# An MLP with seven products a pair: five stage tiles, other request points for weights and blocks, weight sums tied to a bank's addition, operands made one product ahead

## The chip, the core and the metric

The kernel runs on one core of one Trainium2 chip. The metric is the device time of one execution in microseconds (us); several executions give a median. A profile of one execution is read beside it.

## What is computed

The reference is a chain of layers on 1024 tokens of width 1024: a sliding-window attention layer, a pooling layer, then a block with neighbourhood attention and a gated linear recurrence, and at the end of that block an MLP and a norm. The change touches what comes after the recurrence, that is the last lines:

```python
mix = jax.nn.sigmoid(gate_na) * y_na + jax.nn.sigmoid(gate_hg) * y_hg
h = h + mix @ w_o[l]
m = rms_norm(h, norm_mlp[l])
h = h + jnp.square(jax.nn.relu(m @ w_up[l])) @ w_down[l]      # w_up 1024x4096, w_down 4096x1024
h = rms_norm(h, norm_final)
```

All is float32. A product of two float32 matrices is made of three TensorE passes: each operand is split into a high part (a cast on ScalarE) and a low part (operand less high part), and high x high, high x low and low x high are added in a bank of PSUM.

## The kernel before

**The up-projection.** The tokens are halved (Xa, Xb: 512 each), the 1024 input features are halved, and the 4096 output features are taken as 16 pairs of 2 x 128. A pair is a 2x2 matrix product of blocks and is made with seven products in place of eight: A11, A12, S2, S1, S3, S4, A22. Each is four contraction steps of three matmuls 128x128x512, so 12 matmuls, 84 a pair. The activations are ready once for all pairs (`xx`: the parts A11, A12, A22, S1; `sh`: S2 to S4, made by `sums(j)`, L1441 to L1461, from transposes of Xb). For each pair the weights r1 and r2 (raw, 128 x 8 x 128 each) come by DMA (`raws`, L1485); VectorE makes four sums of halves of them (`vec`, L1479: first r2 in place, then the two halves of `tt`, last half of r1 in place); `split_group` (L1470 to L1476) splits r1, tt, r2 and the rest of r1 on ScalarE (`whi`, L1474, ring of three tiles) and GpSimd (`wlo`, L1475). S2 and S1 use tt, S3 and S4 use r2, A22 uses r1's second half, A11 and A12 use all of r1 as it came.

**What follows a product.** A bank is copied out to a stage tile (`copy_out`, ScalarE, L1390), a later bank is added to that tile (`add_bank`, VectorE, L1394), relu and square are two passes of ScalarE (`activated`, L1411 and L1412), and the result goes to DRAM. So u11 = A11, plus A12; u12 = S2's bank plus S4's; u22 = S1's bank plus S3's; u21 = A22's bank. S3 goes on in the bank that u12's copy is read from, so it waits for that copy (L1390); A22 goes on in the bank that u22's addition reads (L1394). At the end of `pair` four sums of u's are made by VectorE (L1479, st<-st) and stored by SyncE's queue (L1518 to L1524) for the second matrix product. Stage tiles are a ring of ten.

**The order.** The code of a pair stands in one order, a scheduler sets the order of instructions on each engine. On VectorE the pieces of one pair stand so: four u sums of the pair before; u11's addition; four weight sums of the next pair; u22's addition; u12's addition. Each engine runs its queue in order, so the weight sums, when their DMA is late, hold up u22's addition. The raw weights of pair p+2 are asked for at the end of `pair(p)`, ahead of its four stores in the code; the tiles must be free.

Pairs 0 to 3 have A11 and A12 early (`first_two` between the `sums(j)`), so their run is five products each. Ahead of all this, GpSimd adds high and low parts of Xa's transposed half back to float32 (eight additions into `fa`, L1432), and `norms(6, 2)` normalises the last of Xb.

**The down-projection.** Four chunks of seven products, 48 matmuls each (`times`). `split_a` and `split_b` make the operands (L117, L118), `less` differences of weights (L1600), `into` adds four banks to X in SBUF (L1640). In the code a product's `into` stands ahead of the next product's operands.

Of the kernel before, what the change touches and what calls it, by code (L numbers as in the profile page):

```python
# [8 lines left out]
F32 = mybir.dt.float32  # L9
# [9 lines left out]
P = 128  # L19
# [10 lines left out]
def fused_kernel(tc, a, out, stop=None, dbg=None):  # L30
# [1262 lines left out]
    xa, xb = x0p.tile([P, 4, D], F32, name="Xa"), x1p.tile([P, 4, D], F32, name="Xb")  # L1293
# [10 lines left out]
    def bank():  # L1304
        return psm.tile([P, 512], F32, name="mm")
# [17 lines left out]

    with ExitStack() as ph:
        gp = ph.enter_context(tc.tile_pool(name="gp", bufs=2))

        def mixed(e):

            mx, wh = [], pair_cols(w_hg, e)
            for i in range(2):  # L1330
                m_h = gp.tile([P, T], F32R, name="mh", bufs=4)
                m_l = gp.tile([P, T], F32R, name="ml", bufs=4)
                mx.append((m_h, m_l))
                for hf in range(2):
                    sl = slice(hf * 512, hf * 512 + 512)
                    sg = []
                    for src in (d_gate[8 + e + i], d_y[e + i]):
                        g_ = gp.tile([P, 512], F32, name="sg", bufs=8)
# [16 lines left out]
        def last_hook(t):  # L1355
            nc.sync.dma_start(out=d_x[t], in_=X[ALL, t, slice(0, D)])
            if t == 5:
                norms(0, 4)
            if t == 6:
                transposed(lambda k: bank(), [X[ALL, i, slice(0, D)] for i in range(4)], g_mlp, xx, 0)  # L1360
# [25 lines left out]
    H0, H1 = slice(0, 512), slice(512, 1024)  # L1386

# [4 lines left out]

    def add_bank(c_, ps):
        nc.vector.tensor_tensor(out=c_, in0=c_, in1=ps, op=ALU.add)  # L1394
        return c_

    with ExitStack() as ph:
# [29 lines left out]
        fa = xa.rearrange("p t (a c) -> p (t a) c", a=2)  # L1427
# [7 lines left out]
        def turned(k):  # L1435
            ps = bank()
            for i in range(4):
                nc.tensor.transpose(ps[:, i * P:(i + 1) * P], xb[:, i, k * P:(k + 1) * P], ident)
            return ps

        def sums(j):  # L1441

            pa, pb = turned(j), turned(4 + j)
# [15 lines left out]
            split_evac(sh[3][0][:, j, :], sh[3][1][:, j, :], s3, nc.gpsimd)  # L1459
            nc.vector.tensor_tensor(out=s2, in0=fa[:, 4 + j, :], in1=s2, op=ALU.subtract)  # L1460
# [24 lines left out]
        def raws(p):  # L1485
            rs = [wp2.tile([P, KT, P], F32, name="raw") if p else raw() for _ in range(2)]
            for r_, i in zip(rs, (0, 1)):
                nc.sync.dma_start(out=r_, in_=cols(w_up, (2 * p + i) * P)[1])
            return rs

        def pair(p, r1, r2):
# [4 lines left out]
            vec(r2[:, lo_], r2[:, lo_], r2[:, hi_], ALU.subtract)  # L1496
            vec(tt[:, lo_], r1[:, lo_], r2[:, lo_], ALU.subtract)
            vec(tt[:, hi_], r2[:, hi_], tt[:, lo_], ALU.subtract)
            vec(r1[:, hi_], r1[:, hi_], tt[:, lo_], ALU.subtract)
# [18 lines left out]
            nc.sync.dma_start(out=d_u["S3"][:, p, :], in_=s3)  # L1518
            s1 = vec(u21, u21, u22, ALU.add)
            nc.sync.dma_start(out=d_u["S1"][:, p, :], in_=s1)  # L1520
            s2 = vec(stage(), u22, s3, ALU.add)
            nc.sync.dma_start(out=d_u["S2"][:, p, :], in_=s2)
            s4 = vec(stage(), u12, s2, ALU.subtract)
            nc.sync.dma_start(out=d_u["S4"][:, p, :], in_=s4)  # L1524
            return nxt

        rs = {0: raws(0), 1: raws(1)}
        for p in range(NPR):
            rs[p + 2] = pair(p, *rs.pop(p))


    with ExitStack() as ph:
# [3 lines left out]
        blocks = [xa[:, 2 * i:2 * i + 2, :].rearrange("p t (a c) -> p (t a) c", a=2) for i in range(2)]  # L1536
# [28 lines left out]
        NCH = NPR // 4  # L1565
        wd = w_dn.rearrange("(q j p) c -> p q j c", j=2, p=P)
        seq = [(c, s_) for c in range(NCH) for s_ in ("A11", "A12", "S2", "S1", "S4", "S3", "A22")]

        def load_a(n):
            if n < len(seq):  # L1570
                c, s_ = seq[n]
                nc.sync.dma_start(out=blocks[n % 3], in_=d_u[s_][:, 4 * c:4 * c + 4, :])

        def load_w(dst, j, n, c):
            for i in range(2):
                q = 4 * c + 2 * i
                nc.sync.dma_start(out=dst[i], in_=wd[:, q:q + 2, j, n * 512:n * 512 + 512])
            return dst

        def load_w11(c):  # L1580
            return load_w([wpool.tile([P, 1024], F32, name="wraw", bufs=3).rearrange("p (k c) -> p k c", k=2)
                           for _ in range(2)], 0, 0, c)

        def load_w21(c):
            return load_w([bb.tile([P, 2, 512], F32, name="wb") for _ in range(2)], 1, 0, c)

        def load_w2(c):
            wx = xt.tile([P, KT, 512], F32, name="xh1")
            w12, w22 = [[wx[:, 4 * n + 2 * i:4 * n + 2 * i + 2, :] for i in range(2)] for n in range(2)]
            load_w(w22, 1, 1, c)  # L1590
            load_w(w12, 0, 1, c)
            return w12, w22
# [33 lines left out]
        load_a(0)  # L1626
        w11 = load_w11(0)
        load_a(1)
# [6 lines left out]
        load_x(1, 0)  # L1635
        for c in range(NCH):
            def into(banks, h, ch, done=False):
                for t in range(4):
                    dst = X[:, 4 * h + t, ch * 512:ch * 512 + 512]
                    nc.vector.tensor_tensor(out=dst, in0=dst, in1=banks[t], op=ALU.add)  # L1640
                    if done and c == NCH - 1:
                        half_done(4 * h + t, ch)
                        if ch == 1 - h:
                            finish(4 * h + t)

            n = 7 * c
            B, A_, C = [[bank() for _ in range(4)] for _ in range(2)] + [None]
            times(B, split_a(n), split_b(w11), True)
            into(B, 0, 0)
            less(w12, w12, w22)  # L1650
            times(A_, split_a(n + 1), split_b(w21), True)
            into(A_, 0, 0, True)
# [4 lines left out]
            less(w11, w22, w11)  # L1657
            C = [bank() for _ in range(4)]
            times(C, split_a(n + 3), split_b(w11), True)
            into(C, 1, 1)  # L1660
            if c < NCH - 1:
# [4 lines left out]
            times(C, split_a(n + 4), split_b(w22), False)  # L1666
            into(C, 0, 1, True)
            times(B, split_a(n + 5), split_b(w12), False)
            into(B, 1, 1, True)
            if c < NCH - 1:  # L1670
                w12, w22 = load_w2(c + 1)
            times(B, split_a(n + 6), split_b(w21), False)
            into(B, 1, 0, True)
            if c < NCH - 1:
                w21 = w21_
    ctx.close()
# [25 lines left out]
```

## Time and profile before

| | us |
|---|---|
| median of three executions (2424.01 to 2425.98) | 2425.92 |
| the profiled execution | 2424.15 |
| its span in the profile | 2422.1 |
| TensorE (PE) busy | 2328.9 (96%) |
| VectorE (DVE) busy | 1438.3 (59%) |
| ScalarE (ACT) busy | 954.0 (39%) |
| GpSimd (POOL) busy | 770.0 (32%) |
| mean granted TensorE clock | 0.992 |

The profiled execution's time is 2.05 us longer than its span, and 1.8 us under the median. Matmuls overlap, so a busy share of 96% is not 96% of the peak: the distance between the starts of two matmuls is what counts.

### The profile page before, as it was taken

To read this page: it belongs to the slowest core of one execution; us is meant where nothing else is said; L and a number is where in the kernel's file an instruction comes from. 1 tells how busy PE (TensorE), PEld (TensorE's weight loads), DVE (VectorE), ACT (ScalarE), POOL (GpSimd) and SP (SyncE) were. 2 spreads that over 40 slices of the span, in tenths; PEclk is the share of its full clock that TensorE was granted. 3 is DMA by queue.
4 is the path that set the end of the run, shared out by engine and by line. 5 is a ranking of instruction groups with operands and counts; after the bars stand their busy time and mean duration, and the time that the engine had idled before them with its cause. 6 is when DMAs were issued, how large, how long until landed. Compare 5 with 4: busy or idle time off the path is not lost. (4 is left out here: it accounts for less than half of the span.)

```text
span 2422.1 us, 32164 instructions
## 1 busy us (share of the span) xinstructions
PE 2328.9 (96%) x12102; PEld 1930.0 (80%) x12102; DVE 1438.3 (59%) x2647; ACT 954.0 (39%) x1783; POOL 770.0 (32%) x519
## 2 busy tenths in 40 slices
PE   8999999999999999999999999999889899899997
PEld 7877778888877888889888888888767777788885
DVE  5566676644457255552474655766864444687776
ACT  5344451422226355542333323322554444433334
POOL 2111132121235443331221211112554344444454
PEclk9999999999999999999999999999999999999999
DMA  5111113111114311211112112663344444754231
GB/s 157 36 27 36 27 36 106 31 57 44 57 61 140 82 47 53 55 61 45 53 36 66 44 44 74 199 236 105 130 152 161 138 140 140 267 193 174 98 120 70
DMA packets 234012, 230.01 MB, mean 95 GB/s; under 512 B 59833, under 2 KB 174863, under 8 KB 230273
## 3 DMA queue, kind: packets, MB, share of 16 engines
q1 hardware_dynamic: 225040, 210.31, 27.3%
q10 hardware_dynamic: 8224, 16.00, 1.8%
q0 software_dynamic: 592, 1.65, 0.3%
q8 instruction: 95, 1.56, 0.3%
q14 instruction: 61, 0.49, 0.1%
HBM read 168.68 MB, written 59.24 MB: 94 GB/s over the span
## 5 line engine op out<-in xcount | busy, mean ns | idle before, releaser
L107 PE MATMUL mm<-xh,whi 128*128 128x512 f32 (+2 forms) x1744 | 673.1, 386 | 18.1 <-DVE st L1394 13.4
L109 PE MATMUL mm<-xl,whi 128*128 128x512 f32 (+2 forms) x1744 | 666.3, 382 | 0.0
L110 PE MATMUL mm<-xh,wlo 128*128 128x512 f32 (+2 forms) x1744 | 663.0, 380 | 2.0 <-POOL wlo L79 2.0
L79 POOL TENSOR_TENSOR wlo<-wraw,whi 128x1024 fp32r<-128x1024 f32 (+1 forms) x134 | 319.0, 2386 | 943.1 <-ACT whi L78 891.4
L107 PEld LDWEIGHTS mm<-xh,whi 128*128 128x128 f32 x1744 | 329.7, 189 | 83.7 <-DVE st L1394 18.6
L110 PEld LDWEIGHTS mm<-xh,wlo 128*128 128x128 f32 x1744 | 330.0, 189 | 66.2 <-POOL wlo L79 3.2
L109 PEld LDWEIGHTS mm<-xl,whi 128*128 128x128 f32 x1744 | 329.9, 189 | 56.0 <-DVE xl L118 0.3
L78 ACT CAST whi<-wraw 128x1024 fp32r<-128x1024 f32 (+1 forms) x134 | 137.2, 1028 | 386.1 <-PE mm L109 165.2
L110 PE MATMUL mm<-whi,xl 128*128 128x512 f32 (+1 forms) x624 | 222.2, 356 | 0.0
L107 PE MATMUL mm<-whi,xh 128*128 128x512 f32 (+1 forms) x496 | 173.2, 349 | 5.1 <-DVE X L1640 3.9
L109 PE MATMUL mm<-wlo,xh 128*128 128x512 f32 (+1 forms) x496 | 172.6, 348 | 0.6 <-POOL wlo L79 0.6
L110 PEld LDWEIGHTS mm<-whi,xl 128*128 128x128 f32 x624 | 118.5, 190 | 16.8
L1479 DVE TENSOR_TENSOR st<-st 128x512 f32<-128x512 f32 x64 | 80.8, 1284 | 84.0 <-ACT st L1412 82.8
L1475 POOL TENSOR_TENSOR wlo<-raw,whi 128x1024 fp32r<-128x1024 f32 (+1 forms) x42 | 88.9, 2117 | 95.8 <-ACT whi L1474 95.7
L107 PE MATMUL mm<-whi,xl 128*128 128x512 f32 x288 | 113.2, 393 | 4.2 <-ACT whi L117 4.0
L109 PE MATMUL mm<-wlo,xl 128*128 128x512 f32 x288 | 112.9, 392 | 2.0 <-POOL wlo L118 2.0
L107 PEld LDWEIGHTS mm<-whi,xh 128*128 128x128 f32 x496 | 94.5, 191 | 17.8 <-issue 4.6
L109 PEld LDWEIGHTS mm<-wlo,xh 128*128 128x128 f32 x496 | 94.4, 190 | 12.2 <-POOL wlo L79 0.8
L110 PE MATMUL mm<-whi,ml 128*128 128x512 f32 x256 | 99.7, 392 | 1.6 <-DVE ml L118 1.6
L107 PE MATMUL mm<-whi,mh 128*128 128x512 f32 x256 | 100.1, 391 | 0.1
L109 PE MATMUL mm<-wlo,mh 128*128 128x512 f32 x256 | 99.9, 390 | 0.0
L1640 DVE TENSOR_TENSOR X<-X,mm 128x512 f32<-128x512 f32 x112 | 73.1, 681 | 37.6 <-PE mm L110 37.6
(343 smaller groups left out, 4372.7 us busy)
## 6 DMA issues: line engine op xcount, KB each, us to landing
wraw<-in_w_in_dram SPq DMA_DIRECT2D x48, 512.0 KB, 3.9
d_S<-st SPq DMA_DIRECT2D x64, 256.0 KB, 3.7
raw<-in_w_up_dram SPq DMA_DIRECT2D x30, 512.0 KB, 5.0
d_A<-st ACTq DMA_DIRECT2D x48, 256.0 KB, 2.0
Xa<-d_S SPq DMA_DIRECT2D x10, 1024.0 KB, 4.9
wraw<-in_pool_w_in_dram SPq DMA_DIRECT2D x18, 512.0 KB, 4.0
Xa<-d_A SPq DMA_DIRECT2D x9, 1024.0 KB, 4.8
wraw<-in_attn_w_in_dram SPq DMA_DIRECT2D x32, 256.0 KB, 3.3
```

The costliest lines, as they stand in the source:

```text
L78: nc.scalar.copy(out=hv[:, i:i + n], in_=view[:, i:i + n])
L79: nc.gpsimd.tensor_tensor(out=lv[:, i:i + n], in0=view[:, i:i + n], in1=f(hv[:, i:i + n]), op=ALU.subtract)
L107: nc.tensor.matmul(ps, lhsT=lh[0], rhs=rh[0], start=first and i == 0, stop=False, skip_group_check=chain)
L109: nc.tensor.matmul(ps, lhsT=lh[0], rhs=rh[1], start=False, stop=False, skip_group_check=chain)
L110: nc.tensor.matmul(ps, lhsT=lh[1], rhs=rh[0], start=False, stop=last and i == n - 1, skip_group_check=chain)
L1475: nc.gpsimd.tensor_tensor(out=lv, in0=view, in1=f(hv), op=ALU.subtract)
L1479: nc.vector.tensor_tensor(out=out_, in0=x_, in1=y_, op=op)
L1640: nc.vector.tensor_tensor(out=dst, in0=dst, in1=banks[t], op=ALU.add)
```

## The change

- Five stage tiles a pair in place of seven: S3's sum is written over u11, S1's over u21, S4's over u12; only S2's gets a tile of its own.
- The weight sums of pair p+1 may only be issued after u22's addition of pair p (`tc.issue_after(ready.pop(p))`); those of pair 0 after u11's addition of pair 3.
- `load_raw`: r2 of pair p+2 is asked for right after r2 of pair p has been split, r1 of p+2 right after the last split of r1 of pair p; before, both at the end of the pair.
- Xa's first four transposed parts are written to `fa` by ScalarE straight from the transposes' banks; the other four additions stay on GpSimd, one inside each `sums(j)`. The eight staging tiles of the stage before (`sg`) lie in `fa`, and Xa has a pool of its own that closes early.
- In the down-projection `operands(n + 1)` is written ahead of `into` of product n; the first two blocks and the first w11 are asked for inside the last pairs.

```diff
+                    if k < 4:
+                        nc.scalar.activation(out=fa[:, k, :], in_=ps, func=AF.Copy, scale=g_mlp[:, k:k + 1])
...
-        for k in range(KT):
-            h, l = xx.at(k, H0)
-            nc.gpsimd.tensor_tensor(out=fa[:, k, :], in0=f(h), in1=f(l), op=ALU.add)
         norms(6, 2)
...
+            h, l = xx.at(4 + j, H0)
+            nc.gpsimd.tensor_tensor(out=fa[:, 4 + j, :], in0=f(h), in1=f(l), op=ALU.add)
...
-            vec(r2[:, lo_], r2[:, lo_], r2[:, hi_], ALU.subtract)
...
+            with tc.issue_after(ready.pop(p)):
+                vec(r2[:, lo_], r2[:, lo_], r2[:, hi_], ALU.subtract)
+                vec(tt[:, lo_], r1[:, lo_], r2[:, lo_], ALU.subtract)
+                vec(tt[:, hi_], r2[:, hi_], tt[:, lo_], ALU.subtract)
+                vec(r1[:, hi_], r1[:, hi_], tt[:, lo_], ALU.subtract)
...
             g = split_group(r2, KT)
+            n2 = load_raw(p + 2, 1)
             product(b_, "S3", [v[:, lo_] for v in g], False)
             u22 = activated(add_bank(u22, b_))
+            ready[p + 1] = added[0].ins
...
             g = split_group(r1[:, hi_], 4)
+            n1 = load_raw(p + 2, 0)
             product(b_, "A22", g, False)
             u21 = activated(b_)
-            nxt = raws(p + 2) if p + 2 < NPR else None
-            s3 = vec(stage(), u21, u11, ALU.subtract)
...
+            for s_, c_, x_, y_, op in (("S3", u11, u21, u11, ALU.subtract), ("S1", u21, u21, u22, ALU.add),
+                                       ("S2", stage(), u22, u11, ALU.add)):
+                nc.sync.dma_start(out=d_u[s_][:, p, :], in_=vec(c_, x_, y_, op))
+            nc.sync.dma_start(out=d_u["S4"][:, p, :], in_=vec(u12, u12, c_, ALU.subtract))
...
+            times(A_, *ops, True)
             less(w11, w11, w12)
-            times(B, split_a(n + 2), split_b(w11), False)
-            into(B, 0, 1)
+            ops = operands(n + 2, w11)
+            into(A_, 0, 0, last)
+            times(B, *ops, False)
```

VectorE in a middle pair, before: the addition of u11 (L1394), the four weight sums (raw and wraw, L1479), the additions of u22 and u12, then the four sums of u's (st<-st).

```order
L1394 TENSOR_TENSOR st<-st,mm 128x512 [waits DMAHW1_49,PE_49,Activation_49]
L1479 TENSOR_TENSOR raw<-raw 128x512 [waits DMAHW6_49,Pool_49]
L1479 TENSOR_TENSOR wraw<-raw 128x512 [waits DMAHW0_49,DVE_49]
L1479 TENSOR_TENSOR wraw<-raw,wraw 128x512 [waits DVE_49]
L1479 TENSOR_TENSOR raw<-raw,wraw 128x512 [waits Pool_49]
L1394 TENSOR_TENSOR st<-st,mm 128x512 [waits DMAHW3_49,PE_49,Activation_49]
L1394 TENSOR_TENSOR st<-st,mm 128x512 [waits DMAHW2_49,PE_49]
```

The same place now (`add_bank` is L1417, `vec` L1515):

```order
L1417 TENSOR_TENSOR st<-st,mm 128x512 [waits PE_49,Activation_49]
L1417 TENSOR_TENSOR st<-st,mm 128x512 [waits DMAHW0_49,PE_49,Activation_49]
L1515 TENSOR_TENSOR raw<-raw 128x512
L1515 TENSOR_TENSOR wraw<-raw 128x512 [waits DMAHW3_49,DVE_49]
L1515 TENSOR_TENSOR wraw<-raw,wraw 128x512 [waits DVE_49]
L1515 TENSOR_TENSOR raw<-raw,wraw 128x512 [waits Pool_49]
L1417 TENSOR_TENSOR st<-st,mm 128x512 [waits DMAHW7_49,PE_49]
L1515 TENSOR_TENSOR st<-st 128x512 [waits DMAHW5_49,Activation_49]
L1515 TENSOR_TENSOR st<-st 128x512 [waits DMAHW1_49,DVE_49]
L1515 TENSOR_TENSOR st<-st 128x512 [waits DMAHW2_49]
L1515 TENSOR_TENSOR st<-st 128x512 [waits DMAHW7_49,DVE_49]
```

The addition of u22 has moved from behind the weight sums to ahead of them; u12's stands behind them as before.

VectorE at the last `sums(j)`, j = 3, before: u11's addition of pair 3, then the sums of activations (L1448, L118, L1460); the first row of raw already belongs to pair 1, since pair 0's weight sums stood 27 rows and more ahead.

```order
L1394 TENSOR_TENSOR st<-st,mm 128x512 [waits PE_49,Activation_49]
L1448 SCALAR_TENSOR_TENSOR st<-mm,vecs,Xa 128x512 [waits PE_49]
L1448 SCALAR_TENSOR_TENSOR st<-mm,vecs,st 128x512 [waits DVE_49,PE_49,Pool_49]
L1448 SCALAR_TENSOR_TENSOR st<-mm,vecs,st 128x512 [waits Activation_49]
L1479 TENSOR_TENSOR raw<-raw 128x512 [waits DMAHW2_49]
L118 TENSOR_TENSOR s2l<-st,s2h 128x512 [waits Activation_49]
```

The same place now; wraw<-wraw are pair 0's four weight sums:

```order
L1417 TENSOR_TENSOR st<-st,mm 128x512 [waits PE_49,Activation_49]
L1482 SCALAR_TENSOR_TENSOR st<-mm,vecs,fa 128x512 [waits PE_49]
L1515 TENSOR_TENSOR wraw<-wraw 128x512 [waits DMAHW6_49,DMAHW5_49,DMAHW7_49,DMAHW4_49,DMAHW1_49]
L1482 SCALAR_TENSOR_TENSOR st<-mm,vecs,st 128x512 [waits DVE_49,PE_49,Pool_49]
L1482 SCALAR_TENSOR_TENSOR st<-mm,vecs,st 128x512 [waits Activation_49]
L1515 TENSOR_TENSOR wraw<-wraw 128x512 [waits DMAHW4_49,DMAHW7_49,DMAHW1_49,DVE_49]
L119 TENSOR_TENSOR s2l<-st,s2h 128x512 [waits Activation_49]
L119 TENSOR_TENSOR xl_15937<-st,xh_15936 128x512 [waits Activation_49]
L1482 SCALAR_TENSOR_TENSOR xl_15937<-mm,vecs,xh_15936 128x512 [waits Activation_49]
L1496 TENSOR_TENSOR st<-fa,st 128x512 [waits DVE_49]
L1515 TENSOR_TENSOR wraw<-wraw 128x512
L1515 TENSOR_TENSOR wraw<-wraw 128x512 [waits DMAHW3_49]
```

Pair 0's weight sums have moved from inside `sums(0)` and `sums(1)` into `sums(3)`.

## Rows read from the trace of the kernel before

**Rows 1.** Waits of PE in 1827 to 2086: total, times, longest.

```profile
PE mm L107 <- DVE st L1394: 11.3, 10, 2.1
PE mm L107 <- ACT st L1390: 11.2, 11, 1.1
```

**Rows 2.** Timeline of PE: start, duration, operation, idle time before and its releaser.

```profile
2015.81 0.50 PE L107 MATMUL mm<-s3h,whi 128*128 128x512 f32 x1 [1.07 <-ACT st L1390]
2016.15 0.40 PE L109 MATMUL mm<-s3l,whi 128*128 128x512 f32 x1
2016.38 0.39 PE L110 MATMUL mm<-s3h,wlo 128*128 128x512 f32 x1
...
2022.69 0.50 PE L107 MATMUL mm<-xh,whi 128*128 128x512 f32 x1 [1.15 <-DVE st L1394]
```

**Rows 3.** Timeline of DVE in that pair and the one before.

```profile
1997.25 0.69 DVE L1479 TENSOR_TENSOR raw<-raw 128x512 f32<-128x512 f32 x1 [5.66 <-DMA raw<-in_w_up_dram]
...
2007.18 5.62 DVE L1479 TENSOR_TENSOR st<-st 128x512 f32<-128x512 f32 x4 [5.99 <-ACT st L1412]
2012.71 0.68 DVE L1394 TENSOR_TENSOR st<-st,mm 128x512 f32<-128x512 f32 x1
2019.29 0.69 DVE L1479 TENSOR_TENSOR raw<-raw 128x512 f32<-128x512 f32 x1 [5.90 <-POOL wlo L1475]
...
2021.95 1.28 DVE L1394 TENSOR_TENSOR st<-st,mm 128x512 f32<-128x512 f32 x2
```

**Rows 4.** SP's queue: the request of r2.

```profile
2013.24 0.41 SPq L1488 DMA_DIRECT2D raw<-in_w_up_dram  x1
```

**Rows 5.** Landing of raw weights, from the view of line L1488, 1985 to 2020.

```profile
DMA to landing us min/median/max: 4.6/4.7/5.7
```

**Rows 6.** Timeline of ACT in that pair.

```profile
2002.38 1.05 ACT L1474 CAST whi<-wraw 128x1024 fp32r<-128x1024 f32 x1 [0.45 <-ACT st L1412]
...
2013.43 0.63 ACT L1411 ACTIVATE st<-st 128x512 f32<-128x512 f32 x1 [3.66 <-DVE st L1394]
...
2015.17 0.58 ACT L1390 COPY st<-mm 128x512 f32<-128x512 f32 x1 [0.45 <-DMA d_S<-st]
```

**Rows 7.** Timeline of POOL in that pair.

```profile
2006.69 2.40 POOL L1475 TENSOR_TENSOR wlo<-raw,whi 128x1024 fp32r<-128x1024 f32 x1 [0.77 <-ACT whi L1474]
2009.84 1.68 POOL L1475 TENSOR_TENSOR wlo<-raw,whi 128x512 fp32r<-128x512 f32 x1 [0.74 <-ACT whi L1474]
2016.78 2.41 POOL L1475 TENSOR_TENSOR wlo<-raw,whi 128x1024 fp32r<-128x1024 f32 x1 [5.26 <-ACT whi L1474]
```

**Rows 8.** DMA issues, 1900 to 2086: count, KB each, median us to landing.

```profile
d_A<-st ACTq DMA_DIRECT2D x25, 256.0 KB, 2.0
```

**Rows 9.** Timeline of DVE in the last two `sums(j)`.

```profile
1760.52 2.43 DVE L118 TENSOR_TENSOR s2l<-st,s2h 128x512 fp32r<-128x512 f32 x1
1762.87 1.76 DVE L118 TENSOR_TENSOR xl<-st,xh 128x512 fp32r<-128x512 f32 x1
...
1766.23 0.67 DVE L1394 TENSOR_TENSOR st<-st,mm 128x512 f32<-128x512 f32 x1
```

**Rows 10.** Timeline of PE: S3 of pair 0, A22 of pair 3.

```profile
1772.26 0.50 PE L107 MATMUL mm<-s3h,whi 128*128 128x512 f32 x1
...
1827.82 0.50 PE L107 MATMUL mm<-xh,whi 128*128 128x512 f32 x1 [2.12 <-DVE st L1394]
```

**Rows 11.** A stretch in pair 0: us, PE busy, granted clock, DMA share, GB/s.

```profile
1765.00:1770.00 5.00, 4.38 (x10) 0.66 1.22 292
```

**Rows 12.** Start of the down-projection: DVE.

```profile
2108.66 3.07 DVE L1640 TENSOR_TENSOR X<-X,mm 128x512 f32<-128x512 f32 x5
2111.64 1.22 DVE L1600 TENSOR_TENSOR wraw<-wraw,xh 128x1024 f32<-128x1024 f32 x1
```

**Rows 13.** The same place on PE.

```profile
2114.05 0.80 PE L107 MATMUL mm<-whi,xl 128*128 128x512 f32 x1 [2.88 <-ACT whi L117]
2116.87 0.79 PE L109 MATMUL mm<-wlo,xl 128*128 128x512 f32 x1 [2.02 <-POOL wlo L118]
```

More of the change, by code (lines that the diff above doesn't have):

```diff
@@ L1 @@
+import itertools
 from contextlib import ExitStack
@@ L1322, in norms, with turned @@
                 nc.vector.tensor_scalar_mul(xn[j], xn[j], r[:, j:j + 1])
+    H0, H1 = slice(0, 512), slice(512, 1024)
+    def turned(half, k):
+        ps = bank()
+        for i in range(4):
+            nc.tensor.transpose(ps[:, i * P:(i + 1) * P], half[:, i, k * P:(k + 1) * P], ident)
+        return ps
     with ExitStack() as ph:
         gp = ph.enter_context(tc.tile_pool(name="gp", bufs=2))
+        sgs = itertools.count()
         def mixed(e):
@@ L1483, in raw, with load_raw, pair @@
             return wpool.tile([P, 1024], F32, name="wraw", bufs=3).rearrange("p (k c) -> p k c", k=KT)
[L1485 to L1491, printed above, removed]
+        def load_raw(p, i):
+            if p >= NPR:
+                return None
+            r_ = wp2.tile([P, KT, P], F32, name="raw") if p else raw()
+            nc.sync.dma_start(out=r_, in_=cols(w_up, (2 * p + i) * P)[1])
+            return r_
+        def pair(p, r1, r2, before_sums=None):
             lo_, hi_ = slice(0, 4), slice(4, 8)
@@ L1513, in pair @@
             g = split_group(r1[:, hi_], 4)
+            n1 = load_raw(p + 2, 0)
             product(b_, "A22", g, False)
             u21 = activated(b_)
-            nxt = raws(p + 2) if p + 2 < NPR else None
-            s3 = vec(stage(), u21, u11, ALU.subtract)
[L1518 to L1528, printed above, removed]
+            if before_sums:
+                before_sums()
+            for s_, c_, x_, y_, op in (("S3", u11, u21, u11, ALU.subtract), ("S1", u21, u21, u22, ALU.add),
+                                       ("S2", stage(), u22, u11, ALU.add)):
+                nc.sync.dma_start(out=d_u[s_][:, p, :], in_=vec(c_, x_, y_, op))
+            nc.sync.dma_start(out=d_u["S4"][:, p, :], in_=vec(u12, u12, c_, ALU.subtract))
+            return n1, n2
+        ready = {0: added[0].ins}
+        rs = {p: [load_raw(p, i) for i in range(2)] for p in range(2)}
+        for p in range(NPR - 1):
+            if p == NPR - 2:
+                load_a(0)
+                load_a(1)
             rs[p + 2] = pair(p, *rs.pop(p))
+        w11 = load_w11(0)
+        pair(NPR - 1, *rs.pop(NPR - 1))
     with ExitStack() as ph:
@@ L1563, in finish @@
                 nc.scalar.dma_start(out=out[tsl, 512:], in_=X[:, t, 512:])
[L1565 to L1582, printed above, removed]
         def load_w21(c):
-            return load_w([bb.tile([P, 2, 512], F32, name="wb") for _ in range(2)], 1, 0, c)
+            return load_d([bb.tile([P, 2, 512], F32, name="wb") for _ in range(2)], 1, 0, c)
         def load_w2(c):
@@ L1635, in fused_kernel, with into, operands @@
         load_x(1, 0)
-        for c in range(NCH):
[L1637 to L1648, printed above, removed]
+        def into(banks, h, ch, done=False):
+            for t in range(4):
+                dst = X[:, 4 * h + t, ch * 512:ch * 512 + 512]
+                nc.vector.tensor_tensor(out=dst, in0=dst, in1=banks[t], op=ALU.add)
+                if done:
+                    half_done(4 * h + t, ch)
+                    if ch == 1 - h:
+                        finish(4 * h + t)
+        def operands(n, b_):
+            return split_a(n), split_b(b_)
+        ops = operands(0, w11)
+        for c in range(NCH):
+            n, last = 7 * c, c == NCH - 1
+            B, A_ = [[bank() for _ in range(4)] for _ in range(2)]
+            times(B, *ops, True)
+            ops = operands(n + 1, w21)
+            less(w12, w12, w22)
             into(B, 0, 0)
-            less(w12, w12, w22)
-            times(A_, split_a(n + 1), split_b(w21), True)
-            into(A_, 0, 0, True)
+            times(A_, *ops, True)
             less(w11, w11, w12)
-            times(B, split_a(n + 2), split_b(w11), False)
-            into(B, 0, 1)
+            ops = operands(n + 2, w11)
+            into(A_, 0, 0, last)
+            times(B, *ops, False)
             less(w21, w21, w11)
             less(w11, w22, w11)
+            ops = operands(n + 3, w11)
+            into(B, 0, 1)
             C = [bank() for _ in range(4)]
-            times(C, split_a(n + 3), split_b(w11), True)
-            into(C, 1, 1)
-            if c < NCH - 1:
+            times(C, *ops, True)
+            ops = operands(n + 4, w22)
+            if not last:
                 w11 = load_w11(c + 1)
```

75 lines of the change are left out of this document (46 added, 29 removed).

## The prediction, made before the changed kernel had run

> **What bounds the kernel now.** I read the engines' busy table first: TensorE is busy 96% of the span, so only its waits and its clock can be won. The change touches the last 700 us alone, so I listed TensorE's waits there by line. From the end of pair 3 to the start of the down-projection there are only two kinds [rows 1]: 10 waits of 11.3 us in all for VectorE's `add_bank` (A22 goes on in the bank that u22's addition reads) and 11 of 11.2 us for ScalarE's `copy_out` (S3 goes on in the bank that u12's copy reads). That is 22.5 us in the 12 pairs 4 to 15, nearly one of each a pair, about 1.1 us each. A restart costs a little more: after a wait the second matmul starts 0.34 us behind the first, and later ones 0.23 us behind each other [rows 2], so 0.11 us a wait. At 0.23 us a product of 12 matmuls takes 2.75 us, a pair 19.3 us.
>
> Then the timelines of one pair, to see why both come late. **A22's wait**: S3 is done at about 2018.6, but u22's addition runs at 2021.95 [rows 3], because the weight sums stand ahead of it on VectorE and start at 2019.29, after 5.9 us of idling. The row names GpSimd there; one pair earlier the same wait of 5.66 us names the DMA of the raw weights [rows 3]. r2 is asked for at 2013.24 [rows 4], and such a load takes 4.6 to 5.7 us [rows 5], so 2018 to 2019: the load is what sets it. **S3's wait**: u12's copy runs at 2015.17 behind relu and square of u11, which start at 2013.43 [rows 6], when u11's addition of 2012.71 is done; that one stands behind the four u sums that took 5.62 us from 2007.18 [rows 3]. Clean sums take 0.69 each, 2.8 us for four; these ran beside two GpSimd splits, 2006.69 to 2009.09 and 2009.84 to 2011.52 [rows 7].
>
> **The change, part by part.** I count time t from the start of a pair's A22 on an unbroken TensorE: A11 of the next pair starts at 2.75, A12 5.5, S2 8.25, S1 11.0, S3 13.75, S4 16.5, the next A22 19.25.
>
> *Requests and the tie.* The requests move 10 us and more ahead of the need: r2 of p+2 needs only r2's split of p, a whole pair before its sums. So the load no longer sets the sums; a load of 5.7 us has a pair's 19 us. The tie puts u22's addition first on VectorE. It starts when S3 is done, 16.6, and ends at 17.3, so A22 has 1.9 us of slack. A22's wait goes. What is late next: the weight sums run from 17.3 to 20.1; the cast of tt (1.05 [rows 6]) after the third sum ends at 20.5, its GpSimd split (2.4 [rows 7]) at 22.9, and S2 needs it at 27.5. Behind the tied sums u12's addition waits until 20.1, and u12 is wanted only for its store and the u sums. Cost nothing; cover 4.6 us.
>
> *u sums.* ScalarE now casts r2 of the next pair ahead of u21's relu. It waits for the ring of `whi` until A22 is done (2.75), takes 3.0 to 4.05, so u21's relu and square are 1 us later (4.1 to 5.4), but GpSimd's split of r2 is over at 6.5 where it used to run beside the sums. The four sums run from 6.5 at the latest to 9.2; the last split of r1 waits for A12 and starts at 9.2. Then u11's addition to 9.9, relu and square to 11.2, the store's issue, u12's copy to about 12.2: S3 at 13.75 has 1.5 us of slack. Were the sums still 5.62 us long, the copy would end at 15.1 and S3 be 1.3 us late, as now: this is the step that I trust least.
>
> *Five stage tiles.* S4's sum over u12 has to wait until u12's store has been read. The store is issued at about 4.1 behind the cast and lands in 2.0 us [rows 8], 6.1; the sum comes at 8.5. If it took as long as a raw load, 5.7 us, the sum would end at 10.5, and S3's slack of 1.5 would still cover it. Nothing; the bound is 0 to 0.3 us a pair. Two pairs of tiles instead of 1.4 in the ring take waits away that no row of PE shows: 0.
>
> So **both waits of the middle pairs go: 22.5 + 21 x 0.11 = 24.8 us**; bounds 12.4 (only A22's) and 24.8.
>
> *Pair 0.* Its weight sums come as late as `sums(3)` now. In exchange GpSimd's splits of tt and r2 no longer run beside `sums(2)`, where two VectorE operations took 2.43 and 1.76 us instead of 0.68 [rows 9], 2.8 us. u11's addition of pair 3, done at 1766.9 [rows 9], should be done between 1761 (its product's end) and 1764. From there ten VectorE operations of 0.65 us up to the third weight sum, the cast and the split: 6.6 + 1.05 + 2.4 = 10 us, so S2 of pair 0 can go on at 1771 to 1774, S1 is done 5.5 us later, plus some 1.7 us, since TensorE has stood for 10 us and here too came back at the lower level of 1.2 GHz: mean granted clock 0.66 over five us after a shorter stop [rows 11]. S3 starts at 1778 to 1781 instead of 1772.26 [rows 10]: 6 to 9 us lost. From S3 of pair 0 to A22 of pair 3 it took 55.6 us [rows 10] where three pairs of five products and two products need 3 x 13.7 + 5.5 = 46.6; with 0.7 us a pair for tt's chain (addition 0.7, three sums 2.1, cast 1.05, split 2.4: 6.2 against 5.5 us of S4 and A22) 48.7: 6.9 us won. Sum 0 to +2, against it about 1 us from eight GpSimd additions less before the last norm: **0**, bounds -4 and +6.
>
> *Xa's parts.* Four more ScalarE operations of 0.7 us beside transposes: hidden by VectorE's work on the same banks; part of the 1 us above.
>
> *Down-projection.* At its start w11's difference `less` runs at 2111.64 behind five additions [rows 12], and TensorE waits 2.88 and 2.02 us for the cast and the split of it [rows 13]. Now it stands behind four and both halves come together: one addition of 0.61 us earlier. **-0.6**, bounds 0 and -2. Later products keep their order but for one or two rows: 0.
>
> **Sum**: 2424.15 - 24.8 - 0 - 0.6 = 2398.75, so **2399 us**. The profiled run lies 1.8 us under the median of 2425.92; I leave that in the range.
>
> **Rivals.** (1) *Half.* The u sums stay slow, S3's wait stays: 11.2 + 11 x 0.11 = 12.4 less, 2411. For it: they collide with two splits now; against it: r2's split is drawn ahead. (2) *Pair 0 dearer.* It loses 9 and pairs 1 to 3 win nothing: 2399 + 8 = 2407. For it: the long stop and the clock. (3) *Both*, 2419 and up: the same time, the change giving back what it takes. (4) *Slower.* The weight sums, now right behind u22's addition, run beside a split in every pair, at 2.43 us [rows 9] instead of 0.69. Then u12's addition is 7 us later; 1.5 us of ScalarE's pause before the cast of r2 and S3's slack of 1.5 cover 3 of them, S3 is 4 us late, 12 x 4.1 = 49: 2448. It decides from 12 x 2.1 us on, that is at sums of about 2 us each. Against it: the split of r1 starts when S1 is done, 13.75, and is over at 17.4; the splits of tt come only after the sums.
>
> The rule beside this rival: the Trainium skill, "SBUF — State Buffer", section "SBUF: two separate sides", says that a VectorE operation with two SBUF inputs and a GpSimd operation exclude each other over one pair of ports, the later one blocked until the whole instruction of the other is done. The trace agrees for the u sums: 5.62 us for four beside splits that kept their 2.40 and 1.68 us. By it one late split costs up to 2.4 us once, not four times: 2399 + 0 with the slack of 1.9 and 1.5, and rival 4 needs four splits in a row, which is why I give it little.
>
> **Chances.** Forecast 0.60 (own range 2391 to 2406), half 0.13, pair 0 dearer 0.08, both 0.09, slower 0.10. 2388 to 2414 holds the first three, 0.81. A difference under 0.2%, 4.9 us, can't be told from none: faster 0.81, same 0.09, slower 0.10.
>
> **What would show it.** Right: in 1827 to 2086 no wait of PE for L1417 or L1411 over 0.2 us, A22 to A22 some 19.4 us; u22's addition right behind S3's end; weight sums of 0.69 with no idling for DMA; u sums under 3.5 us. Pair 0's S3 some 6 us later against the end of `sums(3)`'s transposes, pairs 1 to 3 about 14.3 us apart. Wrong: u sums at 5 us and a wait of about 1 us at each S3 (rival 1); TensorE idle over 12 us before S2 of pair 0 (rival 2); weight sums over 2 us each (rival 4); a wait of S4's sum for DMA, which I put at nothing.

## The result, and the profile after

The changed kernel took 2399.36 us (median; 2398.74 to 2400.93) where the kernel before took 2425.13 us beside it (2424.01 to 2425.98). The ratio is 0.9895, with a 95% interval of 0.9878 to 0.9912. The forecast of 2399 us and its range held. How well its parts held is another matter: two of the reasons behind it were wrong, and the experiments below show in which way.

The profiled execution took 2398.74 us, with a span of 2396.8 us. Its line of engines on the page:

```profile
PE 2320.8 (97%) x12102; PEld 1932.1 (81%) x12102; DVE 1413.3 (59%) x2647; ACT 960.7 (40%) x1787; POOL 758.8 (32%) x515
```

TensorE's waits by line in the last 1000 us, the view of rows 1 over a longer stretch (total, times, longest):

```profile
PE mm L108 <- ACT whi L1510: 12.4, 1, 12.4
PE mm L1335 <- DVE Xb L1328: 4.4, 1, 4.4
PE mm L108 <- DVE X L1662: 4.2, 4, 3.7
PE mm L111 <- POOL wlo L1511: 3.7, 4, 1.7
PE mm L108 <- ACT whi L118: 2.2, 1, 2.2
PE mm L110 <- POOL wlo L119: 2.0, 1, 2.0
```

And in 1827 to 2086 alone, exactly the stretch of [rows 1], one line is left of 22.5 us:

```profile
PE mm L108 <- DVE st L1417: 0.3, 1, 0.3
```

Both waits of the middle pairs have gone. In exchange there is one long wait of 12.4 us: the product S2 of pair 0 waits for the cast of `tt` (L1510).

To see where the time went I cut the last 700 us of both traces at three matmuls: the first of S3 of pair 0, the first of A22 of pair 3 and the first of S3 of pair 15. In the windows (us, PE busy, granted clock, DMA share, GB/s) the kernel before has

```profile
1730.00:1772.20 42.20, 31.68 (x130) 0.88 0.36 100
1772.20:1827.80 55.60, 48.66 (x204) 0.97 0.49 161
1827.80:2079.80 252.00, 231.49 (x984) 1.00 0.42 141
2079.80:2422.10 342.30, 318.71 (x1380) 0.97 0.43 155
```

and the changed kernel

```profile
1730.00:1781.30 51.30, 31.36 (x127) 0.77 0.35 103
1781.30:1830.40 49.10, 47.14 (x205) 1.00 0.49 156
1830.40:2055.30 224.90, 224.90 (x986) 1.00 0.48 162
2055.30:2396.80 341.50, 319.78 (x1381) 0.96 0.42 153
```

| Stretch | before, us | after, us | change | forecast |
|---|---|---|---|---|
| up to S3 of pair 0 | 1772.26 | 1781.32 | +9.1 | +6 to +9, less 1 for the norm |
| S3 of pair 0 to A22 of pair 3 | 55.56 | 49.08 | -6.5 | -6.9 |
| A22 of pair 3 to S3 of pair 15 | 252.00 | 224.88 | -27.1 | -24.8 |
| S3 of pair 15 to the end | 342.28 | 341.52 | -0.8 | -0.6 |
| sum | | | -25.3 | -25.4 |

The third row is more than the whole gain, and the other three add up to +1.8 us: TensorE is busy in every one of the 224.9 us. A pair took 21.5 us on average there and now takes 19.19 us, each like the one before.

One pair on VectorE, the timeline that answers [rows 3] (start, duration, operation, idle time before and its releaser):

```profile
1969.74 3.90 DVE L1515 TENSOR_TENSOR st<-st 128x512 f32<-128x512 f32 x4 [3.51 <-ACT st L1456]
1973.56 0.68 DVE L1417 TENSOR_TENSOR st<-st,mm 128x512 f32<-128x512 f32 x1
1981.48 0.69 DVE L1417 TENSOR_TENSOR st<-st,mm 128x512 f32<-128x512 f32 x1 [7.24 <-issue]
1982.09 0.68 DVE L1515 TENSOR_TENSOR raw<-raw 128x512 f32<-128x512 f32 x1
1982.81 0.69 DVE L1515 TENSOR_TENSOR wraw<-raw 128x512 f32<-128x512 f32 x1
1983.54 0.69 DVE L1515 TENSOR_TENSOR wraw<-raw,wraw 128x512 f32<-128x512 f32 x1
1984.14 0.68 DVE L1515 TENSOR_TENSOR raw<-raw,wraw 128x512 f32<-128x512 f32 x1
```

u22's addition (1981.48) starts when its bank is ready, the four weight sums follow without a gap, and nothing waits for a DMA. The four u sums take 3.90 us instead of 5.62.

The same pair on ScalarE, against [rows 6]:

```profile
1967.50 1.05 ACT L1510 CAST whi<-raw 128x1024 fp32r<-128x1024 f32 x1
1968.46 0.59 ACT L1455 ACTIVATE st<-mm 128x512 f32<-128x512 f32 x1
...
1974.28 0.63 ACT L1455 ACTIVATE st<-st 128x512 f32<-128x512 f32 x1 [0.59 <-DVE st L1417]
...
1976.03 0.59 ACT L1411 COPY st<-mm 128x512 f32<-128x512 f32 x1 [0.45 <-PE mm L111]
```

r2's cast stands ahead of u21's relu now. u12's copy ends at 1976.62, and S3 goes on at 1978.51 from S1 without a break, so the copy has 1.9 us to spare.

### The profile page after: what moved, and what is told of

It reads as the page before. It is cut to its first block, busy times and chain, and to the rows that moved or that the text cites. A ratio compares the mean times of both kernels' runs of the same rounds, so it can differ in the third digit from the quotient of the medians.

```text
span 2396.8 us, 32165 instructions
## 1 busy us (share of the span) xinstructions
PE 2320.8 (97%) x12102; PEld 1932.1 (81%) x12102; DVE 1413.3 (59%) x2647; ACT 960.7 (40%) x1787; POOL 758.8 (32%) x515
## 4 chain that ended last, share of the span: by engine, by line
PE 84%; DVE 9%; issue 3%; ACT 2%; DMA 1%; POOL 1%; SPq 0%; DVEq 0%; ACTq 0%; POOLq 0%
PE mm L111 25%; PE mm L110 25%; PE mm L108 25%; PE A L1129 2%; PE PT L441 1%; PE S L423 1%; PE PT L893 1%; PE S L870 1%; DVE xl L119 1%; DVE r L132 1%; PE tp L1149 1%; DVE s L882 1%; DVE sum L632 1%; DMA d_y<-gate 0%; PE tp L175 0%
## 5 line engine op out<-in xcount | busy, mean ns | idle before, releaser
L110 PEld LDWEIGHTS mm<-wlo,xh 128*128 128x128 f32 x496 | 94.6, 191 | 12.2 <-POOL wlo L80 0.8
L1515 DVE TENSOR_TENSOR st<-st 128x512 f32<-128x512 f32 x64 | 64.8, 1033 | 54.0 <-ACT st L1456 53.0
```

Source lines behind the costliest of these rows:

```text
L110: nc.tensor.matmul(ps, lhsT=lh[0], rhs=rh[1], start=False, stop=False, skip_group_check=chain)
L1515: nc.vector.tensor_tensor(out=out_, in0=x_, in1=y_, op=op)
```

## The experiments

The theory on record: A22's wait came from a load asked for too late, S3's wait from GpSimd's split beside the u sums; requests, tie and early cast each take a part of that away, and pair 0 pays for the tie. The rivals: the tie does all of it, or the requests do. The runs separate the edits in both directions: one part alone in the kernel before, or one part undone in the changed kernel. Each ratio is against the kernel before, run beside them on the same chip: 2425.72 us for b_tie, b_requests, untie_all and untie0, and 2428.03 us for late_requests, tie_u11, cast_late and half_tt. Medians of the two groups are therefore compared by their ratios, and by the time of a pair in the traces. A number in brackets is the pair, as in S3(10).

### The tie alone (b_tie)

In the kernel before:

```diff
     def add_bank(c_, ps):
-        nc.vector.tensor_tensor(out=c_, in0=c_, in1=ps, op=ALU.add)
+        added[:] = [nc.vector.tensor_tensor(out=c_, in0=c_, in1=ps, op=ALU.add)]
...
+            with tc.issue_after(ready.pop(p)):
...
             u22 = activated(add_bank(u22, b_))
+            ready[p + 1] = added[0].ins
```

> The kernel before, with the tie alone: weight sums of pair p+1 after u22's addition of pair p, pair 0's after u11's addition of pair 3. Requests, seven stage tiles, Xa's parts and the down-projection as before. Theory (the order on VectorE and ScalarE that the tie brings sets both waits; loads asked for at the old place land at about 15.7 us after A22's start, before the sums' 17.3): both middle waits go, pair 0 loses its 9 us, 2399 to 2402 us. Rival (the late load of r2 is the cause): the sums still wait for it behind u22's addition, tt and u12 come late, 2410 us or more.

Measured: 2401.51 us (2400.13 to 2404.12), ratio 0.9902 [0.9887, 0.9917]. A pair takes 19.19 us, as in the changed kernel, and between 1840 and 2050 TensorE waits for nothing. So the tie alone gives nearly the whole gain, without the requests, the five tiles and the new down-projection.

### The requests alone (b_requests), and the changed kernel without any tie (untie_all)

b_requests, from the kernel before:

```diff
             g = split_group(r2, KT)
+            n2 = load_raw(p + 2, 1)
...
             g = split_group(r1[:, hi_], 4)
+            n1 = load_raw(p + 2, 0)
...
-            nxt = raws(p + 2) if p + 2 < NPR else None
```

untie_all, from the changed kernel:

```diff
-            with tc.issue_after(ready.pop(p)):
+            with nullcontext():
```

> The kernel before, with the early requests of the raw weights alone. Theory: the weight sums run right behind u11's addition without waiting, so u22's addition is on time and A22's waits (11.3 us) go; the order on ScalarE is the old one, r2's split on GpSimd still runs beside the u sums, S3's waits (11.2 us) stay: about 2411 us. Rival (the late loads cause both waits): about 2397 us, since pair 0 is not delayed either.

> The changed kernel without any tie. Theory: A22's wait is gone by the requests, S3's wait of about 1.2 us comes back in 12 pairs (14 us more), pair 0 wins its 9 us back: about 2403 us. Rival (the tie does nothing but cost pair 0): 2390 us.

Measured: b_requests 2420.75 us (2418.39 to 2425.0), ratio 0.9979 [0.997, 0.9989]; untie_all 2419.63 us (2418.52 to 2422.17), ratio 0.9976 [0.9967, 0.9986]. Both missed what was expected, by 10 and 17 us: the early requests are worth about 5 us alone. A pair takes 21.2 us in b_requests and 21.1 us in untie_all, and both waits of [rows 1] are there. In 1740 to 2100, where the kernel before waits 14.8 us for L1390 and 13.4 us for L1394, b_requests has

```profile
PE mm L107 <- ACT st L1390: 16.2, 13, 2.8
PE mm L107 <- DVE st L1394: 6.2, 10, 1.7
```

and untie_all (L1411 and L1417 are the same two lines)

```profile
PE mm L108 <- ACT st L1411: 12.4, 11, 2.0
PE mm L108 <- DVE st L1417: 6.8, 11, 1.7
```

The timelines tell why. First the weight sums on VectorE in b_requests:

```profile
1970.97 0.69 DVE L1479 TENSOR_TENSOR raw<-raw 128x512 f32<-128x512 f32 x1 [0.49 <-DMA raw<-in_w_up_dram]
1976.28 0.69 DVE L1479 TENSOR_TENSOR wraw<-raw 128x512 f32<-128x512 f32 x1 [4.62 <-DMA raw<-in_w_up_dram]
```

r2 is there in time, but the second sum also reads r1 and now stands 4.62 us for that one. SP's queue in b_requests shows both requests:

```profile
1966.21 0.38 SPq L1490 DMA_DIRECT2D raw<-in_w_up_dram  x1
...
1969.91 0.32 SPq L1527 DMA_DIRECT2D d_S<-st  x1
1970.32 0.42 SPq L1490 DMA_DIRECT2D raw<-in_w_up_dram  x1
```

and in the kernel before, in the same pair:

```profile
1965.32 0.38 SPq L1488 DMA_DIRECT2D raw<-in_w_up_dram  x1
...
1969.02 0.32 SPq L1524 DMA_DIRECT2D d_S<-st  x1
1969.44 0.41 SPq L1488 DMA_DIRECT2D raw<-in_w_up_dram  x1
```

The kernel before asks for r1 first, and there it is the first sum, on r2, that waits. So the edit exchanged the two requests and moved neither out of the way: one stands ahead of the four stores of the u sums, the other behind them, 4.1 us later. The first cannot come earlier than a tile is free: in b_requests GpSimd's split that reads the old r2 runs until 1966.18 ...

```profile
1963.78 2.40 POOL L1475 TENSOR_TENSOR wlo<-raw,whi 128x1024 fp32r<-128x1024 f32 x1 [0.78 <-ACT whi L1474]
```

... and the request follows at 1966.21. There are four such tiles, so a tile of pair 12 is one of pair 10.

Counting requests and sums from pair 1 on shows what I had not seen before the prediction, all for pair 12's weights:

| | second request | its weight sums begin | S3(10) | S3(12), their use |
|---|---|---|---|---|
| before | 1969.44 | 1975.45 | 1972.01 | 2015.81 |
| b_requests | 1970.32 | 1970.97 | 1972.90 | 2015.26 |
| after | 1955.90 | 1982.09 | 1959.32 | 1997.70 |

The kernel before did the sums of pair p+2 ahead of u22(p)'s addition, 40 us before S3 used them and 6 us after the request. (The text on the order ahead of the prediction calls them the sums of the next pair; it is the pair after next.) The request stands 2.6 us ahead of S3(10) before and 3.4 us after: it hardly moved. These are the first of the sums before, on VectorE, and the second request after, on SP's queue:

```profile
1975.45 0.69 DVE L1479 TENSOR_TENSOR raw<-raw 128x512 f32<-128x512 f32 x1 [5.86 <-POOL wlo L1475]
```

```profile
1955.90 0.38 SPq L1526 DMA_DIRECT2D raw<-in_w_up_dram  x1
```

What moved are the sums: 3.4 us after S3(10) before, 22.8 us after it now, that is one pair later, behind u22(11)'s addition.

Rows of this wait name GpSimd's split of r1 in some pairs and the DMA in others, because the two end close together. The DMA is what ends it: for pair 13 the second request went out at 1991.44 and landed 5.7 us later, at 1997.14, and the first sum began at 1997.25 [rows 3], while the split of 1994.98 ran until 1997.39.

### Requests as late as before, with the tie (late_requests)

In the changed kernel:

```diff
-            n2 = load_raw(p + 2, 1)
...
-            n1 = load_raw(p + 2, 0)
             product(b_, "A22", g, False)
             u21 = activated(b_)
+            n1, n2 = load_raw(p + 2, 0), load_raw(p + 2, 1)
```

> The changed kernel with both raw weights of pair p+2 asked for at the end of pair p, as before. Theory (with the sums a pair later the place of the request doesn't matter): 2399 us. Rival (the new request points are part of the gain): 2402 us or more.

Measured: 2402.04 us (2398.99 to 2405.03), ratio 0.9894 [0.988, 0.9909], 19.19 us a pair, no wait in the middle pairs. The median alone would fall to the rival, but the kernel before is 2.9 us slower in this group than beside the changed kernel (2428.03 against 2425.13), the changed kernel's ratio is the same (0.9895), and the middle pairs take the same 224.88 us from A22(3) to S3(15). With the tie in place the early requests are worth nothing there: the sums now stand a whole pair further behind the requests.

### Sums ahead of u22's addition, but only one pair early (tie_u11)

This separates two readings of the tie: that u22's addition has to be first on VectorE, or that the sums must not be a pair ahead of their load. From pair 4 on the sums are tied to u11's addition of the pair before, so they stand ahead of u22's addition, as in the kernel before, but one pair later.

```diff
                 open_[p] = first_two(p, split_group(r1, KT))
+                ready[p + 1] = added[0].ins
...
-            ready[p + 1] = added[0].ins
+            ready.setdefault(p + 1, added[0].ins)
```

> The changed kernel, from pair 4 on with the weight sums of pair p+1 tied to u11's addition of pair p instead of u22's. They then stand ahead of u22's addition again, as before the change, but for the next pair and not for the one after it; on ScalarE the cast of r2 stands behind u21's relu again. Theory (before the change the sums stood a pair too early, so that r2's load could not be there, since its tile is freed only by the split two pairs before): no waiting for DMA, u22's addition on time, no wait of A22; S3's waits are back by the order on ScalarE: 2415 us. Rival (A22's wait went because u22's addition stands ahead of the sums): both waits back, 2425 us or more.

Measured: 2406.19 us (2405.26 to 2409.31), ratio 0.991 [0.9894, 0.9927], 19.83 us a pair. Better than either side expected: A22's waits are away although the sums still stand ahead of u22's addition. What remains is S3's wait, between 1840 and 2050:

```profile
PE mm L108 <- ACT st L1411: 3.2, 10, 0.7
```

No sum waits for a DMA. The fourth waits for GpSimd's split of r1, which reads the half that it overwrites, and u22's addition still starts in time for A22:

```profile
1968.74 0.69 DVE L1515 TENSOR_TENSOR raw<-raw,wraw 128x512 f32<-128x512 f32 x1 [3.78 <-POOL wlo L1511]
1969.35 0.68 DVE L1417 TENSOR_TENSOR st<-st,mm 128x512 f32<-128x512 f32 x1
1971.14 0.69 DVE L1417 TENSOR_TENSOR st<-st,mm 128x512 f32<-128x512 f32 x1 [1.11 <-PE mm L111]
```

So the lateness came from sums a pair ahead of need, on tiles that had only just been filled. Their place ahead of the addition costs at most 0.6 us a pair, and not all of that is shown to be theirs: r2's cast stands behind u21's relu in this run too, the u sums take 5.49 us, and that alone costs 0.3 us a pair (cast_late, next). A longer ring of raw tiles in the kernel before would test the same thing from the other side; it was not tried.

### r2's cast behind u21's relu again (cast_late)

This is the step that I trusted least: S3's wait went because r2's split no longer runs beside the u sums.

In the changed kernel, with u21's relu of pair p kept as `relu21[p + 1]`:

```diff
-            g = split_group(r2, KT)
+            with (tc.issue_after(relu21.pop(p)) if p in relu21 else nullcontext()):
+                g = split_group(r2, KT)
```

> The changed kernel, with one more tie on ScalarE alone: the cast of r2 of pair p+1 may be issued only after the relu of u21 of pair p, where it stood before the change. VectorE's order stays as changed. Theory (the early cast is what lets GpSimd finish r2's split ahead of the u sums): the four u sums take 5.6 us again, S3 waits about 1.1 us for ScalarE's copy in some 12 pairs, with the slow restart 1.3 to 1.4 us each: about 2415 us; no wait for u22's addition. Rival (S3's wait went because of what the tie does on VectorE): 2399 us.

Measured: 2405.0 us (2403.81 to 2409.81), ratio 0.991 [0.9896, 0.9925], 19.49 us a pair. The u sums are slow again, and that costs only 0.3 us a pair where 1.3 were expected. On VectorE in cast_late, and in the kernel before:

```profile
1975.16 5.50 DVE L1517 TENSOR_TENSOR st<-st 128x512 f32<-128x512 f32 x4 [3.88 <-ACT st L1458]
```

```profile
1985.38 5.62 DVE L1479 TENSOR_TENSOR st<-st 128x512 f32<-128x512 f32 x4 [5.98 <-ACT st L1412]
```

Set against the start of A22 of the pair (1969.80, 1978.85, and 1964.76 in the changed kernel), the chain that ends at u12's copy reads:

| us from A22's start | before | cast_late | after |
|---|---|---|---|
| u sums begin | 6.53 | 5.36 | 4.98 |
| u sums take | 5.62 | 5.50 | 3.90 |
| u12's copy ends | 15.11 | 13.83 | 11.86 |
| S3 begins | 15.16 | 13.88 | 13.75 |

S3 is due 13.75 us after A22. The copy comes 3.25 us earlier than before: 1.28 of it without the early cast, 1.97 with it. Only 1.4 of the 3.25 was wanted, and the first 1.28 came from u22 being on time: its relu and square, which stand ahead of u12's and u21's on ScalarE, begin 1.74 us ahead of A22's start in cast_late and 0.02 us ahead of it before. In the changed kernel the copy waits for nothing but the end of S2, so an earlier u chain would not bring it forward. The two waits were nearly one: late weight sums made u22 late, A22 waited for it, and the same lateness passed on through the u sums to S3.

### Pair 0 without its tie (untie0)

In the changed kernel:

```diff
-            with tc.issue_after(ready.pop(p)):
+            with (tc.issue_after(ready.pop(p)) if p else nullcontext()):
```

> The changed kernel, but pair 0's weight sums are not tied to u11's addition of pair 3; all other pairs stay tied. Theory (pair 0's tie is what keeps TensorE idle for 12.4 us before S2 of pair 0): its sums go back into the first activation sums, S3 of pair 0 starts at about 1772 as before the change instead of 1781.3, the rest follows 9 us earlier: 2390 us. Rival (the splits of tt and r2 on GpSimd then run beside the last activation sums again and slow them, so little is won): 2395 us or more.

Measured: 2390.92 us (2387.94 to 2393.01), ratio 0.9856 [0.9841, 0.9871]. S3 of pair 0 starts at 1774.85 instead of 1781.32, 6.5 us earlier where 9 were expected, and pairs 1 to 3 are as fast as in the changed kernel (43.7 and 43.6 us from S3(0) to S3(3), 47.8 before). So what those pairs won does not depend on pair 0's tie. It comes with the ties of pairs 1 to 3: b_tie has 43.7 us there, untie_all 46.1. Pair 0's tie costs 6.5 us by the traces and 8.4 us by the medians. In the changed kernel the third weight sum of pair 0 ends at 1770.3, then come the casts, and one after the other GpSimd's splits:

```profile
1770.32 2.51 ACT L1510 CAST whi<-wraw 128x1024 fp32r<-128x1024 f32 x3
```

```profile
1771.98 5.91 POOL L1511 TENSOR_TENSOR wlo<-wraw,whi 128x1024 fp32r<-128x1024 f32 x3
```

```profile
1771.42 0.79 PE L108 MATMUL mm<-s2h,whi 128*128 128x512 f32 x1 [12.36 <-ACT whi L1510]
...
1774.38 0.80 PE L111 MATMUL mm<-s2h,wlo 128*128 128x512 f32 x1 [1.74 <-POOL wlo L1511]
```

### tt's split in halves on top of that (half_tt)

Pairs 1 to 3 still took 14.6 us each against 13.7 for their products: `tt`'s sums, cast and split are the chain there. In untie0 the third matmul of pair 1's S2 still waits for the split:

```profile
1784.38 0.50 PE L111 MATMUL mm<-s2h,wlo 128*128 128x512 f32 x1 [0.62 <-POOL wlo L1511]
```

S2 needs the first half of `tt` alone, so half_tt takes untie0 and casts and splits the first half of `tt`, then the second:

```diff
+        def split_halves(view):
...
+            for s_ in (slice(0, 4), slice(4, 8)):
+                nc.scalar.copy(out=hv[:, s_], in_=view[:, s_])
+                nc.gpsimd.tensor_tensor(out=lv[:, s_], in0=view[:, s_], in1=f(hv)[:, s_], op=ALU.subtract)
...
-            g = split_group(tt, KT)
+            g = split_halves(tt)
```

> The kernel with pair 0 untied, and the split of tt done in two halves (cast and GpSimd split of the first half, which S2 reads, then of the second). Theory (the 0.6 us waits of S2 in pairs 1 to 3 come from the chain addition, three sums, cast, split; halves take 1.6 us from it): those waits go, about 2388.5 us. Rival (two casts and two splits more a pair push other work on ScalarE and GpSimd): the same as untied or worse, 2391 us and up.

Measured: 2388.15 us (2385.68 to 2390.36), ratio 0.9837 [0.9822, 0.9852], against the kernel before on the same chip. From S3(0) to S3(3) it takes 40.95 us instead of 43.73, and the three waits of S2 for `tt`'s split, 1.9 us in all in untie0, are gone. This is the fastest median here, and its interval lies clear of the changed kernel's. Against untie0 the intervals overlap; the 2.8 us in pairs 1 to 3 are shown by the traces.

### Seven stage tiles, and the old order of the down-projection (seven_tiles, old_down)

seven_tiles, from the changed kernel (each sum's store, left out here, follows it as before):

```diff
-            for s_, c_, x_, y_, op in (("S3", u11, u21, u11, ALU.subtract), ("S1", u21, u21, u22, ALU.add),
-                                       ("S2", stage(), u22, u11, ALU.add)):
...
+            s3 = vec(stage(), u21, u11, ALU.subtract)
...
+            s1 = vec(u21, u21, u22, ALU.add)
...
+            s2 = vec(stage(), u22, s3, ALU.add)
...
+            s4 = vec(stage(), u12, s2, ALU.subtract)
```

old_down, from the changed kernel, with `less` and `into` in the old order too:

```diff
-            times(B, *ops, True)
-            ops = operands(n + 1, w21)
+            times(B, *operands(n, w11), True)
...
```

> The changed kernel with S3's and S4's sums in stage tiles of their own again (seven a pair in a ring of ten). Theory (writing over u11 and u12 is worth nothing): a pair is 19.2 us as with five tiles, one look within 5 us of 2399. Rival (the smaller ring use takes waits away): pairs of 19.4 us and more, waits of ScalarE or VectorE for DMA.

> The changed kernel with the down-projection's operands written behind the additions again. Theory (worth one addition of 0.6 us at the first w11): from S3 of pair 15 to the end 0.5 to 1 us more than 341.5 us. Rival (the new order is worth several us): 344 us and more.

Measured, one execution each: 2402.21 us with seven tiles, 2404.35 us with the old down-projection, the kernel before at 2431.09 us beside them. Both have 19.19 us a pair, so the five tiles neither cost nor give anything in the middle pairs. From S3(15) to the end old_down takes 342.5 us. The new order takes 341.5 us in the changed kernel, but 342.5 in late_requests, and the old order 341.9 in b_tie. The scatter is as large as the effect, so the runs do not settle what the down-projection's new order is worth; it is about 1 us at most.

## Why the forecast held, and which of its reasons did not

**Both waits go, and the size.** Right as a result, 24.8 us forecast, 27.1 measured. Two slips in the sum worked against each other, which is in part luck. The 22.5 us of [rows 1] include A22(3)'s wait of 2.12, which ended at 1827.82 [rows 10], ahead of this stretch, and which the term for pair 0 counts as well. The other 20 waits are 20.4 us; by the windows the stretch had 252.00 - 231.49 = 20.5 us of idle time. And a wait costs more than 0.11 us beyond its idle time. The view counts from the modelled end of the matmul before, 0.39 us after its start, where an unbroken TensorE would have gone on 0.23 us after it. On TensorE before, with the wait of [rows 2] behind it:

```profile
2014.36 0.39 PE L110 MATMUL mm<-xh,wlo 128*128 128x512 f32 x1
```

S3 started 1.45 us after this matmul and lost 1.45 - 0.23 = 1.22 us, not 1.07; with the 0.11 of the step behind it that is 0.27 us on top of the idle time. 20 waits x 0.27 = 5.4. The remaining 1.3 us lies in the 944 other steps, 0.2299 us on average before and 0.2285 after: 20.4 + 5.4 + 1.3 = 27.1.

**The load no longer sets the sums.** Right as a result, wrong as a step. "The requests move 10 us and more ahead of the need" is the sentence that failed: the second request of a pair moved by only about 1 us, from 2.6 to 3.4 us ahead of S3(10), since the release of a tile and the stores ahead on SP's queue set the requests. The slack came because the tie moved the need by a pair: late_requests has no wait either. With the requests as the only edit, the same reasoning missed by 10 us (b_requests).

**The tie puts u22's addition first.** Right in its times, but the place is not what counted most: in tie_u11 the sums stand ahead of the addition and A22's waits are away all the same. As for the times, on the prediction's clock the weight sums were to run from 17.3 to 20.1, and from A22 at 1964.76 they ran from 17.3 to 20.1. The 1.9 us of A22's slack are 1.8. One wait of the sign's kind is left, 0.34 us at A22(15), where at most 0.2 was forecast. Rival 4, sums beside a split, did not come: each took 0.68 or 0.69 us.

**u sums.** The order was right (r2's cast 2.7 us after A22's start, 2.75 forecast; the copy's end at 11.9, 12.2 forecast; slack 1.9, 1.5 forecast), the size not quite: 3.90 us where 2.8 were added up and the sign allowed 3.5, since the first sum began beside the split's end. Taken apart on VectorE, with the split on GpSimd under it:

```profile
1969.74 1.84 DVE L1515 TENSOR_TENSOR st<-st 128x512 f32<-128x512 f32 x1 [3.51 <-ACT st L1456]
```

```profile
1968.63 2.41 POOL L1511 TENSOR_TENSOR wlo<-raw,whi 128x1024 fp32r<-128x1024 f32 x1
```

The first sum took 1.84 us instead of 0.69 and ended 0.5 us after the split did at 1971.04; the three behind it took 2.02 together. The prediction's rule from the Trainium skill ("SBUF — State Buffer", section "SBUF: two separate sides") is that the later operation is blocked until the other is done; the trace agrees to 0.2 us, for a sum of 0.69 us begun at the split's end would have ended 0.7 us after it. One reading beside that rule was wrong: the short split of 1.68 us [rows 7] had not kept its time. The same split takes 1.29 us in the changed kernel (at 1973.77), so beside the u sums GpSimd lost 0.4 us as well.

But the conclusion, "were the sums still 5.62 us long, ... S3 be 1.3 us late, as now", failed: cast_late has 5.50 us and S3 is 0.13 us late against its A22. The step took the start of the sums as unchanged, 6.5 us after A22; with u22 on time they start at 5.36 even with the late cast. So rival 1, half of the gain gone, could not have come the way it was put: slow u sums alone do not keep S3's wait.

**Five tiles.** Zero forecast, zero measured (seven_tiles). **Pair 0.** A zero of two large numbers: 9.1 lost against "6 to 9", 6.5 won against 6.9, so +2.6 inside the bounds of -4 and +6. That the loss fits is in part luck: against the last transposes of `sums(3)`, which start at 1760.10 before and 1758.03 now, S3 of pair 0 comes 11.1 us later, not some 6, and the transposes themselves come 2.1 us earlier, where 1 us was put down for them and the last norm. The stop that the forecast named as a sign of rival 2, over 12 us before S2, was there (12.36), yet pairs 1 to 3 kept their gain, so the rival's other half did not come. That pairs 1 to 3 gain without pair 0's tie (untie0) was not seen in the forecast: the two were taken as one exchange. **Down-projection.** -0.6 forecast, -0.8 measured, of which 0.5 is A22(15)'s wait (0.83 us before, 0.34 now), and not told apart from scatter. The two waits of [rows 13] came down from 2.88 and 2.02 to 2.22 and 1.96 us.

## What to carry to other kernels

When a wait names a DMA, look at how far ahead of its use the waiting work stands, not only at when the load was asked for: with a ring of tiles the load cannot start before the old tile is read, and work drawn too far forward in an in-order queue turns that into a stall of whatever is behind it. Two waits that alternate in a loop can be one delay that is passed on, so look for a common cause before you price them apart. Look at the first round of a loop apart too: a tie that is free in steady state cost 6.5 us where the engine had nothing else to run.

## What the runs showed of the hardware

A TensorE wait cost 0.27 us more than the idle time that its row names, with matmuls 0.23 us apart. After the stop of 12.4 us TensorE came back at the lower of its two levels, 1.2 GHz; the windows (us, busy of PE, PEld, DVE, ACT and POOL, granted clock, DMA share, GB/s) of the changed kernel put that at 6.9 us:

```profile
1771.40:1778.30 6.90, 5.14 (x11) 3.64 (x12) 0.00 (x0) 1.43 (x2) 6.48 (x4) 0.50 0.31 128
1778.30:1781.30 3.00, 3.00 (x14) 2.44 (x13) 0.00 (x0) 0.59 (x1) 0.00 (x0) 1.00 0.03 5
```

Eleven matmuls ran in that time, 0.43 us apart where nothing else held them. At 0.23 us each they would have been 11 x 0.20 = 2.2 us shorter by this estimate; the forecast had 1.7 for it. On GpSimd two half splits took 2.59 us (half_tt) where one whole split takes 2.40, so cutting an operation in two cost 0.2 us and let S2 start on its first half.

```profile
1796.12 2.59 POOL L1520 TENSOR_TENSOR wlo<-wraw,whi 128x512 fp32r<-128x512 f32 x2 [6.94 <-ACT whi L1519]
```
